# A decoder layer on one core: the second norm in a written order, and the first gate/up pair from eight block products

## The chip, the cores and the metric

The kernel runs on one NeuronCore of a Trainium2 chip. The metric is the device time of one execution in microseconds (us), lower is better. Five engines work side by side, each through its own list of instructions in order: TensorE (PE; its weight loads are shown as PEld), VectorE (DVE), ScalarE (ACT), GpSimd (POOL) and SyncE (SP), which starts most loads. They wait for each other by semaphores.

## What is computed

One layer of a decoder with 512 positions and a model width of 1024, all in float32:

```
h = rms_norm(x, attn_pre_norm) @ w_in          # split over four kinds of attention, 4 heads each
mix = concatenate([moba, nsa, diff, swa])      # 512 x 1024
x = x + rms_norm(mix @ w_out, attn_post_norm)
h = rms_norm(x, ffn_pre_norm)                  # "the second norm", with the line above
a = causal_conv3(h @ w_gate) + conv_b          # width 4096
x = x + rms_norm((gelu(a) * (h @ w_up)) @ w_down, ffn_post_norm)
```

## The kernel before

Every matrix product is made from float32r operands that are split into a high half (an ACT copy) and a low half (the difference, mostly on DVE), and three matmuls, high x high, high x low and low x high (`mm3`, L396). The weights come in by DMA and are split just ahead of their use; class `Weights` hands their steps to a queue (`later`, `pop`) that is emptied one step at a time between matmuls. The 512 positions are four tiles `t` of 128 rows, the width 1024 two halves `n` of 512.

**Out-projection.** The first half of its depth is made inside the attention (`fill_out`) and copied into `part[t][n]`. The other half needs the last heads: `out_rest(t, n)` (L1162) makes 12 matmuls of 512 columns into one PSUM bank and DVE adds the bank to `part` (L1168). The mixed heads reach it as `mixh` (ACT, L950) and `mixl` (POOL, L951); the last `mixl` ends the attention.

**Second norm** (`second_norm`, L1188; `rstd2`, L1170). Per tile: ACT squares `part` with a running sum, DVE adds the sums, POOL raises to -0.5; `part` is multiplied by the first gain (DVE for tile 0, POOL for the others), DVE multiplies by `r` and adds to `x1` (L1195), then squares, `r` and product with the second gain once more (L1198). `x1` is loaded again from memory by ACT's queue (L1155).

**Gate and up.** 32 column tiles of 128 each are made in 16 pairs. A pair is a product of a 2 x 2 block matrix (weights) with a 2 x 2 block matrix (normed rows, transposed), done by seven block products of 24 matmuls of 256 columns instead of eight; POOL makes the combinations of the weight blocks (L167) and DVE and ACT those of the results (`first_products`, `other_products`). The right operands are the normed rows: `"11"` and `"21"` hold tiles 0 and 1 (first and second 512 features), `"12"` and `"22"` tiles 2 and 3, and `t1` to `t4` are combinations of them (`other_operands`, L1231). `right_operand` (L1200) makes one: eight TensorE transposes, two ACT copies, two DVE subtractions. In front of the rest, `first_products` of pairs 0 and 1 use only `"21"` and `"11"`. Weight operands are split into buffers `wu`; the first two, four halves in all, go to buffers called `wa`.

A scheduler orders each engine's instructions from the program's order, its own estimate of times and priorities (`tc.high_priority`).

## Time and profile before

| | us |
|---|---|
| runs, median of 3 (lowest to highest) | 824.68 (823.82 to 824.93) |
| the profiled execution | 825.51 |
| its span, from the first to the last instruction | 823.7 |
| TensorE busy in the span | 781.1 |
| DVE busy | 659.4 |
| ACT busy | 445.5 |
| POOL busy | 345.2 |

Times in rows are counted from the start of the span. A busy matmul is counted to its modelled end, so neighbours overlap: what a matmul costs is the distance of its start to the next one's start. The order of rows below stands without times, as the program was built.

### The profile page before, as it was taken

The page shows a single profiled execution, that of the slowest core. Times are in us where ns is not written, and L with a number is a line of the kernel's source. Part 1 is how long each engine was busy: PE and PEld are TensorE (multiplying, and loading weights), DVE is VectorE, ACT ScalarE, POOL GpSimd, SP SyncE. Part 2 cuts the span into 40 slices and gives each one's busy share as a digit, 9 for nine tenths or more (in the row PEclk, how much of TensorE's full clock was granted, in tenths as well). Part 3 has the DMA queues.
Part 4 walks back from the last instruction along what each step waited for, and adds up shares of the span by engine and source line. Part 5 has one row for each costly group of instructions (what it writes and reads, how often), then busy time and mean ns, then how long its engine had stood idle before and what let it go on. Part 6 is the DMA issues. An engine that isn't in the chain of part 4 may idle for free.

```text
span 823.7 us, 13488 instructions
## 1 busy us (share of the span) xinstructions
PE 781.1 (95%) x5079; PEld 711.5 (86%) x5079; DVE 659.4 (80%) x1124; ACT 445.5 (54%) x930; POOL 345.2 (42%) x312
## 2 busy tenths in 40 slices
PE   7999998999999779999999999999999999999994
PEld 6998887998877569988998998998998998998983
DVE  4647669777686999995797797897897897899766
ACT  6457656776776535644554454454454454455432
POOL 5136342337344657333433432452451451564005
PEclk9999998999999969999999999999999999999998
DMA  7274211406321403422123314305306216123302
GB/s 225 52 200 128 58 40 45 125 24 204 105 70 56 148 17 113 128 78 77 52 80 125 103 51 155 103 25 182 96 12 200 72 32 204 29 75 103 102 27 102
DMA packets 72920, 78.76 MB, mean 96 GB/s; under 512 B 7782, under 2 KB 58136, under 8 KB 72856
## 3 DMA queue, kind: packets, MB, share of 16 engines
q1 hardware_dynamic: 70888, 73.18, 28.6%
q10 hardware_dynamic: 1968, 4.73, 1.6%
q8 instruction: 40, 0.66, 0.3%
q14 instruction: 24, 0.20, 0.1%
HBM read 73.71 MB, written 2.10 MB: 92 GB/s over the span
## 4 chain that ended last, share of the span: by engine, by line
PE 56%; DVE 32%; DMA 4%; issue 3%; ACT 3%; POOL 2%; SPq 0%; ACTq 0%; DVEq 0%; POOLq 0%
DVE wu L184 13%; PE mm L397 5%; PE mm L398 4%; PE mm L399 4%; PE tr L398 3%; DVE y L1313 3%; PE mm L1263 3%; PE mm L1265 3%; PE mm L1264 3%; PE tr L399 3%; PE sc L1265 3%; PE sc L1264 3%; PE sc L1263 3%; PE tr L397 3%; PE tr L924 2%
## 5 line engine op out<-in xcount | busy, mean ns | idle before, releaser
L184 DVE TENSOR_TENSOR wu<-pair,wu 128x512 fp32r<-128x512 f32 x188 | 176.1, 972 | 15.2 <-ACT wu L181 15.0
L181 ACT ACTIVATE wu<-pair 128x512 fp32r<-128x512 f32 x188 | 108.3, 622 | 74.8 <-PE sc L1265 19.6
L1265 PE MATMUL mm<-fT,wu 128*128 128x256 f32 x488 | 138.3, 283 | 0.7 <-DVE wu L184 0.7
L1263 PE MATMUL mm<-fT,wu 128*128 128x256 f32 x488 | 138.2, 283 | 0.7 <-ACT mo L1294 0.7
L1264 PE MATMUL mm<-fT,wu 128*128 128x256 f32 x488 | 138.2, 283 | 0.0
L142 ACT ACTIVATE wu<-raw 128x512 fp32r<-128x512 f32 (+2 forms) x126 | 71.3, 610 | 78.3 <-DMA raw<-in_ffn_w_down_dram 28.5
L1264 PE MATMUL sc<-fT,wu 128*128 128x256 f32 x392 | 111.3, 284 | 0.0
L1263 PE MATMUL sc<-fT,wu 128*128 128x256 f32 x392 | 111.1, 284 | 0.0
L1265 PE MATMUL sc<-fT,wu 128*128 128x256 f32 x392 | 111.1, 283 | 0.0
L167 POOL TENSOR_TENSOR sum<-pair 128x512 f32<-128x512 f32 x32 | 48.4, 1515 | 140.0 <-DMA pair<-in_ffn_w_up_dram 63.4
L167 POOL TENSOR_TENSOR pair<-sum,pair 128x512 f32<-128x512 f32 x32 | 55.9, 1761 | 117.5 <-DVE wu L184 115.7
L167 POOL TENSOR_TENSOR pair<-pair 128x512 f32<-128x512 f32 x64 | 103.9, 1634 | 2.0
L147 DVE TENSOR_TENSOR wu<-raw,wu 128x512 fp32r<-128x512 f32 (+2 forms) x95 | 67.6, 727 | 38.7 <-ACT wu L142 38.3
L1263 PEld LDWEIGHTS mm<-fT,wu 128*128 128x128 f32 x488 | 93.6, 192 | 1.2 <-ACT mo L1294 0.9
L1265 PEld LDWEIGHTS mm<-fT,wu 128*128 128x128 f32 x488 | 93.6, 192 | 0.9 <-DVE wu L184 0.9
L1264 PEld LDWEIGHTS mm<-fT,wu 128*128 128x128 f32 x488 | 93.6, 192 | 0.3
L1263 PEld LDWEIGHTS sc<-fT,wu 128*128 128x128 f32 x392 | 75.4, 193 | 0.4
L1264 PEld LDWEIGHTS sc<-fT,wu 128*128 128x128 f32 x392 | 75.3, 192 | 0.3
L1265 PEld LDWEIGHTS sc<-fT,wu 128*128 128x128 f32 x392 | 75.3, 192 | 0.0
L892 POOL TENSOR_SCALAR P<-P,rc 128x128 f32<-128x128 f32 (+2 forms) x80 | 43.0, 558 | 75.6 <-DVE rc L990 29.5
L147 POOL TENSOR_TENSOR wu<-raw,wu 128x512 fp32r<-128x512 f32 (+2 forms) x31 | 42.0, 1359 | 55.4 <-ACT wu L142 50.4
L900 ACT ACTIVATE P<-P,mn 128x128 f32<-128x128 f32 (+2 forms) x96 | 52.0, 543 | 21.5 <-DVE mn L899 21.0
(312 smaller groups left out, 1998.6 us busy)
## 6 DMA issues: line engine op xcount, KB each, us to landing
pair<-in_ffn_w_gate_dram SPq DMA_DIRECT2D x16, 1024.0 KB
pair<-in_ffn_w_up_dram SPq DMA_DIRECT2D x16, 1024.0 KB, 5.3
raw<-in_ffn_w_down_dram SPq DMA_DIRECT2D x32, 512.0 KB, 3.8
raw<-in_w_in_dram SPq DMA_DIRECT2D x14, 512.0 KB, 3.7
raw<-in_w_out_dram SPq DMA_DIRECT2D x8, 512.0 KB, 4.2
raw<-in_w_in_dram SPq DMA_DIRECT2D x10, 256.0 KB, 2.7
x<-in_x_dram SPq DMA_DIRECT2D x4, 512.0 KB, 6.2
x<-in_x_dram ACTq DMA_DIRECT2D x4, 512.0 KB, 8.6
```

Of the source, the lines that this page charges most:

```text
L142: self.nc.scalar.activation(box["h"][:, sl], box["r"][:, sl], AF.Copy)
L147: eng.tensor_tensor(box["l"][:, sl], box["r"][:, sl], f32(box["h"][:, sl]), op=ALU.subtract)
L167: self.nc.gpsimd.tensor_tensor(block(g, out), block(g, a), block(g, b), op=op)
L181: self.nc.scalar.activation(box["h"][g], block(g, src), AF.Copy)
L184: self.nc.vector.tensor_sub(box["l"][g], block(g, src), f32(box["h"][g]))
L397: pe.matmul(o, lh, rh, start=first, stop=False)
L398: pe.matmul(o, lh, rl, start=False, stop=False)
L399: pe.matmul(o, ll, rh, start=False, stop=last)
L900: act.activation(pi, pi, AF.Exp, bias=mn[:, i:i + 1], scale=-1.0, accum_out=sm[:, i:i + 1])
L1263: pe.matmul(o, wh, rh, start=first, stop=False, skip_group_check=True)
L1264: pe.matmul(o, wh, rl, start=False, stop=False, skip_group_check=True)
L1265: pe.matmul(o, wl, rh, start=False, stop=last, skip_group_check=True)
```

## The change

- Pair 0 is made from its plain blocks. `add_blocks` splits four operands (11, 12, 21, 22) and no combination of weights; `block_products` makes eight products straight into four PSUM banks, in two rounds, `a = 0` for tiles 0 and 1, `a = 1` for tiles 2 and 3. Pair 1 still takes seven products and comes after pair 0.
- The out-projection's rest, the second norm, the transposes and the products of pair 0 are issued in a written order, which `tc.keep_in_program_order` holds on every engine. `out_rest` is finished one half after the other, tiles 0 and 1 first. The scalar steps of the norm are two POOL operations per norm, the first gain is POOL's for `n = 0` and DVE's for `n = 1`.
- The weights `wa` are split earlier (`ask_ahead`), inside the attention; three instead of four buffers of pair weights are loaded at first; `x1` is loaded by SP's queue.
- Lines move: L167 of before is L174, L184 is L191, L899 is L907, L924 is L932, L951 is L959, L956 is L964; the out-projection is L1196, its add L1198, the gain L1216, the residual L1222, the second product L1227, transposes and low halves of operands L1241 and L1244, block products L1393.

The core of the diff:

```diff
 class Weights:
@@
-        self.spare, self.held = {}, 0
+        self.spare, self.held, self.ahead = {}, 0, set()
+        self.keep = lambda i: i
@@
-    def add_operands(self, u, js, q, late=False):
-        for j in js:
+    def add_operands(self, u, q):
+        for j in range(7):
             n = len(self.units)
-            self.units.append(lambda j=j, n=n: self.operand(u, j, n, q, late))
+            self.units.append(lambda j=j, n=n: self.operand(u, j, n, q, OPERANDS, 6))
+
+    def add_blocks(self, u, q):
+
+        for j in range(4):
+            n = len(self.units)
+            self.units.append(lambda j=j, n=n: self.operand(u, j, n, q, BLOCKS, 3))
 
     def open_pairs(self, pool):
         self.big = pool
-        self.room["pair"] = PAIRS
+        self.room["pair"] = PAIRS - 1
         self.pump()
@@
+    def ask_ahead(self):
+
+        self.ahead = set(self.spare)
+        for u in sorted(self.ahead):
+            self.later(*self.units[u]())
...
@@
+    pair_units(0, W.add_blocks)
+    pair_units(1, W.add_operands)
...
@@
         W.spare = {u: lambda: [tt("wa", "H") for _ in range(2)] for u in W.spare}
+        W.ask_ahead()
         for n in range(2):
@@
+    keep = tc.keep_in_program_order
     x1 = [fp.tile([128, D], F32, name=f"x1_{t}") for t in range(4)]
     for t in range(4):
-        act.dma_start(x1[t], x[0, 128 * t:128 * t + 128, :])
+        sp.dma_start(x1[t], x[0, 128 * t:128 * t + 128, :])
+    W.done("pair")
@@
+    def out_rest(t, n):
+        ps = bank(("mm", "sc")[n])
+        sl = slice(128 * t, 128 * t + 128)
+        for k in range(4):
+            w = ws[2 * n + k // 2]
+            for a, c in ((0, 0), (0, 1), (1, 0)):
+                keep(pe.matmul(ps, mixT[a][4 + k][:, sl], w[c][:, k % 2, :], start=k == 0 and a == c == 0,
+                               stop=k == 3 and a == 1))
+        return lambda: keep(vec.tensor_add(part[t][n], part[t][n], ps))
+
+    def squares(t, n, src):
+
+        if n == 0:
+            rms[t] = (st.tile([128, 2], F32, tag="ssa", name=nm("ss")), st.tile([128, 1], F32, tag="ra", name=nm("r")))
+        ss, r = rms[t]
+        junk = acts.tile([128, 1024], BF16, tag="mo", name=nm("junk"), bufs=MO)
+        keep(act.activation(junk[:, 0:512], src, AF.Square, scale=1.0 / 32, accum_out=ss[:, n:n + 1]))
+        if n == 0:
+            keep(pool.tensor_scalar(r, ss[:, 0:1], 1.0, EPS, ALU.mult, ALU.add))
+        else:
+            keep(pool.tensor_tensor(r, r, ss[:, 1:2], op=ALU.add))
+            keep(pool.tensor_tensor(r, r, mhalf[:, 0:1], op=ALU.pow))
+
+    def first_gain(t, n):
+        keep((pool, vec)[n].tensor_tensor(part[t][n], part[t][n], half_of(gpost, n), op=ALU.mult))
+
+    def residual(t):
+        r = rms[t][1]
         for n in range(2):
             xh = half_of(x1[t], n)
-            vec.scalar_tensor_tensor(xh, part[t][n], r, xh, ALU.mult, ALU.add)
-        r = rstd2(x1[t])
+            keep(vec.scalar_tensor_tensor(xh, part[t][n], r, xh, ALU.mult, ALU.add))
+            squares(t, n, xh)
+
+    def second_norm(t):
         for n in range(2):
-            vec.scalar_tensor_tensor(part[t][n], half_of(x1[t], n), r, half_of(gpre, n), ALU.mult, ALU.mult)
...
+            keep(vec.scalar_tensor_tensor(part[t][n], half_of(x1[t], n), rms[t][1], half_of(gpre, n),
+                                          ALU.mult, ALU.mult))
...
@@
+    half_done(0, 0)
+    half_done(0, 1)
+    residual(0)
+    half_done(1, 0)
+    half_done(1, 1)
+    second_norm(0)
+    residual(1)
+    for n in range(2):
+        for t in (2, 3):
+            adds[t, n] = out_rest(t, n)
+        W.free(2)
+    half_done(2, 0)
+    half_done(3, 0)
+    second_norm(1)
+    R["11"] = right_operand([part[0][0], part[1][0]], operand_tiles("M"), keep)
+    R["21"] = right_operand([part[0][1], part[1][1]], operand_tiles("M"), keep)
+    half_done(2, 1)
+    residual(2)
+    for _ in range(4):
+        pop()
+    half_done(3, 1)
+    residual(3)
+    second_norm(2)
+    for _ in range(4):
+        pop()
+    second_norm(3)
@@
-    firsts = [first_products(tag) for tag in ("mm", "sc")]
-    with tc.high_priority(HN):
-        other_operands()
+    def block_products(j, a, hold):
+
+        wh, wl = first_ws[j]
+        rh, rl = R[("11", "21", "12", "22")[2 * a + j % 2]]
+        for g in range(2):
+            o = first_banks[j // 2, g][:, 256 * a:256 * a + 256]
+            for k in range(4):
+                for n, (l, r) in enumerate(((wh, rh), (wh, rl), (wl, rh))):
+                    hold(pe.matmul(o, l[g][:, k, :], r[k], start=j % 2 == 0 and k == 0 and n == 0,
+                                   stop=j % 2 == 1 and k == 3 and n == 2))
+                if side and a:
+                    pop()
+
+    first_ws = [W.take() for _ in range(4)]
+    first_banks = {(f, g): bank(("mm", "sc")[f]) for f in range(2) for g in range(2)}
+    for j in range(4):
+        if j == 3:
+            R["12"] = right_operand([part[2][0], part[3][0]], operand_tiles("F"), keep)
+            R["22"] = right_operand([part[2][1], part[3][1]], operand_tiles("X"), keep)
+        block_products(j, 0, keep)
...
+    for j in range(4):
+        block_products(j, 1, keep)
+        name, src = others[j]
+        R[name] = right_operand(src, late[name], keep)
+        if j % 2:
+            W.free(2)
+            pend.append(gate_and_up(j // 2, first_banks[j // 2, 0], first_banks[j // 2, 1]))
+    pend += pair_of_tiles(1)
```

How the order moves, at three places.

The end of the attention, DVE and TensorE. `P`, `sc`, `mn`, `rc`, `sm` are softmax tiles, `mo` a pair of heads, `wa` the two early weight operands. DVE before, in a row:

```order
L879 RECIPROCAL rc_2675<-rc_2675 128x4
L899 ISA P_2667,mn_2668<-sc_2707,sbias,nsink 128x256
L899 ISA mn_2668 128x1
L1030 TENSOR_SCALAR rc_2675<-rc_2675,nlam 128x4
L946 TENSOR_TENSOR mo_2695<-vb_2686,tmp_2696 64x512
L899 ISA P_2667,mn_2668<-sc_2715,sbias,nsink 128x256
L899 ISA mn_2668 128x1
L1033 SCALAR_TENSOR_TENSOR P_2507<-P_2590,rc_2675,P_2507 128x128
```

and now:

```order
L191 TENSOR_TENSOR wa_2686<-pair_0_2636,wa_2684 128x512
L191 TENSOR_TENSOR wa_2687<-pair_1_2638,wa_2685 128x512
L907 ISA P_2665,mn_2666<-sc_2712,sbias,nsink 128x256
L907 ISA mn_2666 128x1
L907 ISA P_2665,mn_2666<-sc_2721,sbias,nsink 128x256
L907 ISA mn_2666 128x1
L886 TENSOR_SCALAR rc_2673<-sm_2592 128x4
L954 TENSOR_TENSOR mo_2699<-vb_2690,tmp_2700 64x512
L887 RECIPROCAL rc_2673<-rc_2673 128x4
L191 TENSOR_TENSOR wa_2742<-pair_0_2636,wa_2740 128x512
L1038 TENSOR_SCALAR rc_2673<-rc_2673,nlam 128x4
L191 TENSOR_TENSOR wa_2743<-pair_1_2638,wa_2741 128x512
```

Four subtractions of `wa` stand among the softmax steps; before they stood behind the attention's last row. TensorE before (`kk` and `kl` with `qs` make scores, `mm` is the out-projection's bank):

```order
L956 MATMUL sc_2707<-kk_2657,qs_2383 128x256
L957 MATMUL sc_2707<-kl_2631,qs_2383 128x256
L956 MATMUL sc_2715<-kk_2657,qs_2383 128x256
L957 MATMUL sc_2715<-kl_2631,qs_2383 128x256
L956 MATMUL sc_2738<-kk_2657,qs_2392 128x128
L957 MATMUL sc_2738<-kl_2631,qs_2392 128x128
L399 MATMUL mm_3179<-wu_2957,mixl_2552 128x512
L399 MATMUL mm_3193<-wu_2957,mixl_2552 128x512
L956 MATMUL sc_2759<-kk_2657,qs_2392 128x256
```

and now:

```order
L964 MATMUL sc_2712<-kk_2655,qs_2383 128x256
L965 MATMUL sc_2712<-kl_2631,qs_2383 128x256
L964 MATMUL sc_2721<-kk_2655,qs_2383 128x256
L965 MATMUL sc_2721<-kl_2631,qs_2383 128x256
L1196 MATMUL mm_3169<-wu_2971,mixl_2552 128x512
L964 MATMUL sc_2748<-kk_2655,qs_2392 128x128
L965 MATMUL sc_2748<-kl_2631,qs_2392 128x128
L964 MATMUL sc_2769<-kk_2655,qs_2392 128x256
L965 MATMUL sc_2769<-kl_2631,qs_2392 128x256
```

The matmul with `mixl` stands ahead of one more pair of score matmuls, and belongs to one output half instead of two.

The gate/up products, TensorE: the transposes for tiles 2 and 3 (`part` with numbers 2938, 3010 before; 2952, 3024 now). Before, in the middle of a product:

```order
L1264 MATMUL sc_3482<-fT_3308,wu_3413 128x256
L1265 MATMUL sc_3482<-fT_3307,wu_3413 128x256
L1208 MATMUL tr_3550<-ident,part_2938 128x128
L1263 MATMUL sc_3482<-fT_3298,wu_3413 128x256
L1264 MATMUL sc_3482<-fT_3299,wu_3413 128x256
L1265 MATMUL sc_3482<-fT_3298,wu_3413 128x256
L1263 MATMUL sc_3482<-fT_3298,wu_3413 128x256
L1264 MATMUL sc_3482<-fT_3299,wu_3413 128x256
L1265 MATMUL sc_3482<-fT_3298,wu_3413 128x256
L1208 MATMUL tr_3550<-ident,part_3010 128x128
```

and now, where the third block ends:

```order
L1393 MATMUL sc_3434<-fT_3341,wu_3392 128x256 x2
L1393 MATMUL sc_3434<-fT_3342,wu_3392 128x256
L1393 MATMUL sc_3434<-fT_3341,wu_3392 128x256
L1241 MATMUL tr_3511<-ident,part_2952 128x128
L1241 MATMUL tr_3511<-ident,part_3024 128x128
L1241 MATMUL tr_3511<-ident,part_2952 128x128
L1241 MATMUL tr_3511<-ident,part_3024 128x128
L1241 MATMUL vb_3518<-ident,part_2952 128x128
```

Sixteen transposes now stand in a row ahead of the fourth block; before, products stood between them.

The second norm of tiles 2 and 3, DVE (`x_2`, `x_3` are the residuals of those tiles, `part` the rows, `fT` low halves of right operands, `wu` low halves of weights). Before:

```order
L1195 SCALAR_TENSOR_TENSOR x_3_3171<-part_3010,r_3392,x_3_3171 128x512
L1195 SCALAR_TENSOR_TENSOR x_3_3171<-part_3160,r_3392,x_3_3171 128x512
L1211 TENSOR_TENSOR fT_3281<-tr_3275,fT_3280 128x512
L1211 TENSOR_TENSOR fT_3290<-vb_3284,fT_3289 128x512
L1211 TENSOR_TENSOR fT_3299<-tr_3293,fT_3298 128x512
L1181 TENSOR_SCALAR r_3382<-ss_3379 128x1
L1211 TENSOR_TENSOR fT_3308<-va_3302,fT_3307 128x512
L1181 TENSOR_SCALAR r_3402<-ss_3399 128x1
L1198 SCALAR_TENSOR_TENSOR part_2938<-x_2_3170,r_3382,gains 128x512
L1198 SCALAR_TENSOR_TENSOR part_3109<-x_2_3170,r_3382,gains 128x512
L1198 SCALAR_TENSOR_TENSOR part_3010<-x_3_3171,r_3402,gains 128x512
L1198 SCALAR_TENSOR_TENSOR part_3160<-x_3_3171,r_3402,gains 128x512
```

and now:

```order
L191 TENSOR_TENSOR wu_3392<-pair_0_2636,wu_3392 128x512
L191 TENSOR_TENSOR wu_3392<-pair_1_2638,wu_3392 128x512
L1198 TENSOR_TENSOR part_3148<-part_3148,sc_3310 128x512
L1216 TENSOR_TENSOR part_3148<-part_3148,gains 128x512
L1222 SCALAR_TENSOR_TENSOR x_3_3159<-part_3024,r_3332,x_3_3159 128x512
L1222 SCALAR_TENSOR_TENSOR x_3_3159<-part_3148,r_3332,x_3_3159 128x512
L1227 SCALAR_TENSOR_TENSOR part_2952<-x_2_3158,r_3383,gains 128x512
L1227 SCALAR_TENSOR_TENSOR part_3123<-x_2_3158,r_3383,gains 128x512
L191 TENSOR_TENSOR wu_3416<-pair_0_2636,wu_3416 128x512
L191 TENSOR_TENSOR wu_3416<-pair_1_2638,wu_3416 128x512
L1227 SCALAR_TENSOR_TENSOR part_3024<-x_3_3159,r_3405,gains 128x512
L1227 SCALAR_TENSOR_TENSOR part_3148<-x_3_3159,r_3405,gains 128x512
```

Tile 3's add, gain and residual stand behind the weight halves that follow tile 2's residual; before both residuals stood together, ahead of the low halves of tiles 0 and 1.

## Rows read from the trace of the kernel before

**Rows 1.** Page, engines: busy us (share of the span), instructions.

```profile
PE 781.1 (95%) x5079; PEld 711.5 (86%) x5079; DVE 659.4 (80%) x1124; ACT 445.5 (54%) x930; POOL 345.2 (42%) x312
```

**Rows 2.** Stretches: window, its length, busy us of each engine (instructions), clock, DMA share, GB/s.

```profile
230.00:269.50 39.50, 35.99 (x223) 29.82 (x223) 28.69 (x92) 28.92 (x81) 20.55 (x28) 1.00 0.23 68
269.50:298.50 29.00, 17.56 (x74) 13.38 (x72) 28.97 (x40) 15.29 (x35) 20.05 (x17) 0.81 0.23 90
...
365.00:800.00 435.00, 431.20 (x2928) 399.13 (x2927) 366.70 (x478) 208.68 (x365) 163.10 (x100) 1.00 0.29 94
```

**Rows 3.** TensorE's waits, 230 to 420 us: total, times, longest us.

```profile
PE tr L1208 <- DVE part L1198: 10.0, 2, 6.6
...
PE tr L1208 <- DVE r L1181: 1.0, 1, 1.0
...
PE mm L1263 <- ACT mo L1294: 0.7, 1, 0.7
...
PE vb L1208 <- DVE fT L1211: 0.4, 1, 0.4
```

**Rows 4.** POOL in order of time: start, us, line, operation [idle before].

```profile
268.23 1.30 POOL L951 TENSOR_TENSOR mixl<-mo,mixh 128x512 fp32r<-128x512 f32 x1 [2.64 <-ACT mixh L950]
...
277.13 1.30 POOL L1192 TENSOR_TENSOR part<-part,gains 128x512 f32<-128x512 f32 x1
...
286.81 0.54 POOL L1182 TENSOR_TENSOR r<-r,mhalf 128x1 f32<-128x1 f32 x1 [2.61 <-DVE r L1181]
```

**Rows 5.** TensorE in order of time, out-projection's end, first product, transposes.

```profile
282.65 0.39 PE L398 MATMUL sc<-wu,mixh 128*128 128x512 f32 x1
282.88 0.39 PE L399 MATMUL sc<-wu,mixl 128*128 128x512 f32 x1
...
298.54 0.79 PE L1263 MATMUL mm<-fT,wa 128*128 128x256 f32 x2
...
313.30 0.28 PE L1265 MATMUL sc<-fT,wu 128*128 128x256 f32 x1
313.42 0.28 PE L1263 MATMUL sc<-fT,wu 128*128 128x256 f32 x1
313.54 0.60 PE L1208 MATMUL tr<-ident,t 128*128 128x128 f32 x4
313.89 0.36 PE L1264 MATMUL sc<-fT,wu 128*128 128x256 f32 x1
```

**Rows 6.** DVE in order of time, 269 to 300 us.

```profile
269.30 1.98 DVE L184 TENSOR_TENSOR wa<-pair,wa 128x512 fp32r<-128x512 f32 x3 [1.81 <-ACT wa L181]
...
277.28 3.40 DVE L1195 SCALAR_TENSOR_TENSOR x<-part,r,x 128x512 f32<-128x512 f32 x2
...
285.26 1.40 DVE L1195 SCALAR_TENSOR_TENSOR x<-part,r,x 128x512 f32<-128x512 f32 x2
286.59 0.14 DVE L1181 TENSOR_SCALAR r<-ss 128x1 f32<-128x1 f32 x1
...
298.86 0.68 DVE L1211 TENSOR_TENSOR fT<-tr,fT 128x512 fp32r<-128x512 f32 x1
```

**Rows 7.** ACT in order of time, 268 to 273 us.

```profile
268.63 2.20 ACT L181 ACTIVATE wa<-pair 128x512 fp32r<-128x512 f32 x4 [0.48 <-issue]
272.09 0.63 ACT L1176 ACTIVATE junk<-part 128x512 bf16<-128x512 f32 x1 [1.26 <-DVE part L1168]
272.63 0.19 ACT L1176 ACTIVATION_READ_ACCUMULATOR junk<-part 128x1 f32 x1
```

**Rows 8.** Page, DMA issues: KB each, median us to landing.

```profile
x<-in_x_dram ACTq DMA_DIRECT2D x4, 512.0 KB, 8.6
```

**Rows 9.** Stretches of 1 and 2 us; the clock is third from the end.

```profile
288.00:290.00 2.00, 0.16 (x1) 0.16 (x2) 2.00 (x4) 2.00 (x6) 0.90 (x1) 0.50 0.00 0
132.00:133.00 1.00, 0.00 (x0) 0.00 (x0) 0.97 (x4) 0.98 (x2) 0.01 (x1) 1.00 0.00 0
134.00:135.00 1.00, 0.98 (x5) 0.56 (x4) 1.00 (x3) 1.00 (x4) 0.00 (x0) 0.54 0.99 318
```

More of the change, by code (lines that the diff above doesn't have):

```diff
@@ L180, in hi @@
                                            for a in range(2)] for t in self.slot(n))
-            self.nc.scalar.activation(box["h"][g], block(g, src), AF.Copy)
+            self.keep(self.nc.scalar.activation(box["h"][g], block(g, src), AF.Copy))
         def lo(g):
-            self.nc.vector.tensor_sub(box["l"][g], block(g, src), f32(box["h"][g]))
+            self.keep(self.nc.vector.tensor_sub(box["l"][g], block(g, src), f32(box["h"][g])))
             if g == 1:
                 self.ready[n] = (box["h"], box["l"])
-            if j == 6:
+            if j == last:
                 self.done("pair")
         steps = [lambda: hi(0), lambda: hi(1), lambda: lo(0), lambda: lo(1)]
-        sums = [lambda g=g, m=m: combine(g, *m) for m in (
-            ("s", "21", "22", ALU.add), ("21", "11", "21", ALU.subtract),
-            ("11", "s", "11", ALU.subtract), ("12", "12", "11", ALU.subtract)) for g in range(2)]
-        if j == 2 and late:
-            return sums + steps
-        return steps + sums if j == 1 and not late else steps
+        if j == 1 and srcs is OPERANDS:
+            steps += [lambda g=g, m=m: combine(g, *m) for m in (
+                ("s", "21", "22", ALU.add), ("21", "11", "21", ALU.subtract),
+                ("11", "s", "11", ALU.subtract), ("12", "12", "11", ALU.subtract)) for g in range(2)]
+        return steps
     def ask(self):
@@ L201, in ask @@
             self.split += 1
-            self.later(*self.units[self.split - 1]())
+            if self.split - 1 not in self.ahead:
+                self.later(*self.units[self.split - 1]())
+    def ask_ahead(self):
+        self.ahead = set(self.spare)
+        for u in sorted(self.ahead):
+            self.later(*self.units[u]())
     def take(self):
@@ L285, with sum_tile @@
     W.later, W.pop = later, pop
-    def sum_tile(late):
-        t = tf("sum") if late else wst.tile([128, S], F32, tag="sum", name=nm("sum"), bufs=2)
+    def sum_tile():
+        t = wst.tile([128, S], F32, tag="sum", name=nm("sum"), bufs=2)
         return t.rearrange("p (k c) -> p k c", k=4)
@@ L1160, with half_of @@
     ws = [W.take() for _ in range(4)]
[L1162 to L1168 removed]
+    def half_of(a, n):
+        return a[:, 512 * n:512 * n + 512]
     def rstd2(*src):
@@ L1200, in right_operand, with operand_tiles @@
-    def right_operand(src, tags, tag):
+            keep(vec.scalar_tensor_tensor(part[t][n], half_of(x1[t], n), rms[t][1], half_of(gpre, n),
+                                          ALU.mult, ALU.mult))
+    def operand_tiles(tag):
+        return [t2pool.tile([128, S], F32R, tag="X", name=nm("fT")) if tag == "X" else tt("fT", tag) for _ in range(4)]
+    def right_operand(src, tiles, hold):
         hi, lo = [], []
         for m in range(2):
-            ps = bank(tags[m])
+            ps = bank(("tr", "pv")[m])
@@ L1207, in right_operand @@
                     c = 128 * (2 * m + k)
-                    pe.transpose(ps[:, 256 * k + 128 * u:256 * k + 128 * u + 128], src[u][:, c:c + 128], ident)
-            h, l = (t2pool.tile([128, S], F32R, tag="X", name=nm("fT")) if tag == "X" else tt("fT", tag) for _ in range(2))
-            act.activation(h, ps, AF.Copy)
-            vec.tensor_sub(l, ps, f32(h))
+                    hold(pe.transpose(ps[:, 256 * k + 128 * u:256 * k + 128 * u + 128], src[u][:, c:c + 128], ident))
+            h, l = tiles[2 * m:2 * m + 2]
+            hold(act.activation(h, ps, AF.Copy))
+            hold(vec.tensor_sub(l, ps, f32(h)))
             for k in range(2):
```

103 lines of the change are left out of this document (39 added, 64 removed).

## The prediction

> **What bounds the kernel now.** I read the page's table of engines first, then the stretches, then the waits of TensorE, then single rows in order of time. TensorE is the busiest engine [rows 1], and the stretches say where it is not: from 365 us to 800 it works 431.2 of 435 us, but from 269.5 to 298.5, the second norm, only 17.6 of 29 [rows 2]. The reader is to see two regimes there: a feed-forward part in which every matmul more is paid in full, and a hole of 11.4 us ahead of it in which DVE is busy all the time (28.97 of 29). The waits name the hole: TensorE's transposes of the normed rows (L1208) wait 10.0 us for DVE's L1198, and 1.0 us for a small DVE operation [rows 3]. So only three things can move the time: the matmuls that TensorE has to do, the end of the attention, and the wait between that and the first gate/up product.
>
> I count from M, the end of the last low half of the attention's output (POOL L951, 268.23 + 1.30 = 269.5 us [rows 4]). TensorE starts the first product at 298.54 [rows 5], that is M + 29.0.
>
> **More matmuls.** Pair 0 takes eight block products instead of seven: 24 matmuls of 256 columns more. Two of them in a row start 0.12 us apart (313.30, 313.42): 2.9 us. There are also eight right operands to transpose instead of seven; four transposes take 0.35 us of TensorE (313.54 to 313.89), so eight take 0.7 [rows 5]. All of it lies on the engine that is full: **+3.6**. What pair 0 loses on other engines (eight POOL combinations, five DVE sums, two ACT copies, three weight operands to split) hides beside TensorE before and is worth nothing, but for a wait of 0.7 us on one of those copies (L1294), and a 0.4 us wait on an fT low half in the same stretch, which I expect gone [rows 3]: **-1.1** (bounds -1.1 and 0).
>
> **The end of the attention.** The four halves of two operands called wa were split behind the attention: four ACT copies from 268.63, 2.20 us, and four DVE subtractions, 1.98 us for the first three [rows 6, 7]. Now they stand between the last softmax tiles (first fences of order). Ahead of M, DVE and ACT are busy 28.7 and 28.9 of 39.5 us, 73% [rows 2]. Four subtractions at 0.66 (1.98 / 3) are 2.6; at that share 1.9 us lie on the chain of softmax steps. Worst is copies and subtractions one behind the other, 4 x (0.55 + 0.66) = 4.8. Best is a gain: out-projection matmuls that stood ahead of the last value products no longer do; the twelve of one output half at 0.23 us (282.65 to 282.88 [rows 5]) are 2.8 us, so -2.8. I take **+1.9**, by the row of DVE's share. The four loads of x1 go from ACT's queue to SP's; they land 8.6 us after issue [rows 8], and are first wanted some 7 us behind M while issued about 3 ahead of it, so I cost them at nothing; should they be late, every us is paid at the first norm. SP has them ahead of the second half of pair 1's weights, which nobody needs before pair 1's combinations.
>
> **The first norm.** The out-projection's rest was done for several output tiles side by side, which filled TensorE's gaps in the attention; now each of the eight halves is finished before the next begins. The first half can't end before M, and the other seven follow: 84 x 0.23 = 19.3, with the first half's last matmul M + 19.6. Meanwhile tiles 0 and 1 go through DVE, ACT and POOL. Tile 1's second half leaves TensorE at M + 8.7; add 0.7, square 0.63 + 0.19 [rows 7], two small POOL operations at 0.54 [rows 4] behind a POOL gain of 1.3, residual 1.4 for two [rows 6], two squares 1.6, POOL 1.1, two products 1.4: about M + 17.5, inside the cover. So TensorE goes from the out-projection straight to the transposes, and the first product stands at 19.6 + 0.35 + 0.55 + 0.68 = M + 21.2 (a bank's four transposes, ACT's copy at 2.20 / 4, DVE's low half [rows 6, 7]). Against 29.0: **-7.8**. If the chain is stretched as DVE's steps were beside POOL's gains (below), it is later by 2 to 4 us: bounds -7.8 and -4.
>
> **What is late next: tiles 2 and 3.** On TensorE the transposes of tiles 2 and 3 stand in a row between block 2 and block 3 (second fences), so nothing passes them. Three blocks, 72 matmuls at 0.12, last to 21.2 + 8.6 = M + 29.8. On DVE the order is now fixed (third fences): the four low halves of tiles 0 and 1 end at about M + 22.2 (sixteen transposes are 1.4, a copy and a low half 1.2), and only then tile 2's second half is added. From there one step waits for the next: add 0.7, square 0.8, POOL 1.1, residual 1.4 (M + 26.2); a square 0.8 on ACT, behind it two weight copies 1.1, then the second weight subtraction 0.7 on DVE (28.8); tile 3's add 0.7, square 0.8, POOL 1.1, residual 1.4 (32.8); last square 0.8, two weight copies 1.1, two weight subtractions 1.3, two products 1.4: M + 37.4 (the last POOL pair runs beside the weight halves). Some fifteen hand-overs between engines come on top; DVE's r ends at 286.73 and POOL starts at 286.81 [rows 4, 6], 0.08 each, 1.2 in all: M + 38.6. TensorE waits 38.6 - 29.8 = **+8.8**, first for the third block's weights, then for tile 3. Before, TensorE waited nowhere in this stretch, since two product groups ran while tiles 2 and 3 were normed. Bounds: 1.5, if the scalar steps overlap far better than this row by row sum; 12, if two residuals take 3.40 us instead of 1.40, as they did beside POOL's gains (277.28, 285.26 [rows 6]).
>
> That last pair of rows shows DVE's step as long as POOL's gain of 1.30 and the one after it. The Trainium skill (SBUF — State Buffer, section "SBUF: two separate sides") calls the port that the two share an exclusive lock held for a whole instruction, and the rows agree (1.40 against 3.40). By that rule the chain of tiles 2 and 3 is free of it, since POOL then has only operations of one column, and 8.8 stands; without the rule it would be 8.8 + 2 x 2.0.
>
> **The sum.** +3.6 - 1.1 + 1.9 - 7.8 + 8.8 = +5.4. The profiled execution of before took 825.51 us (span 823.7, 1.8 around it), so 830.9; it lies 0.8 above the median of the three runs, 824.68, which gives **830.1**.
>
> TensorE's clock is at its lower level (0.50, 1.2 GHz) from 288 us on [rows 9], after the long wait; the new wait of about 9 us would cost the same, so I put no term. But TensorE fell to it at 134.5 too, having stood still from 132 to 133 [rows 9].
>
> **Rivals.**
> Faster: the norms of tiles 2 and 3 overlap and TensorE waits only 1.5 us. For it: DVE has less to do in the stretch than before (no sums of pair 0, POOL fewer gains), and the scalar steps are on three engines. Against it: the fixed order puts one tile behind the other. +3.6 - 1.1 + 1.9 - 7.8 + 1.5 = -1.9, 822.8.
> No change: a wait of 3.4 us, in the middle, 824.7.
> Much slower, by one mechanism: TensorE holds its out-projection matmuls in order inside the attention, stands before the low half of a mixed tile, and the score matmuls behind it (the first fences) come late. The attention's chain has hardly slack, so the stall of some 2 us is paid, and the clock falls as at 134.5; six us at half clock would cost up to 3. It decides as soon as that low half is later than the row of matmuls, and gives 830.1 + 5 = 835.1. The Trainium skill (TensorE: Matmul & The Clock Gate, section "HAM oscillation — how this bites in real kernels") says that waits between bursts bring the slow clock back each time; the drop at 134.5 agrees.
>
> **Chances.** Forecast 0.55; much slower 0.20; faster 0.16; no change 0.09. 0.2% (1.6 us) is about what a measurement of this kernel can tell from no change. Of the forecast's own range, 826.5 to 833.5, all is slower. The range reaches to the faster case's centre and just past the slowest's: 822.5 to 836. Faster by over 0.2% 0.16, within 0.09, slower 0.75.
>
> **What would show it.** First product behind the last L951 (now L959) by 21 to 23 us instead of 29.0; 24 matmuls and 8 transposes more; TensorE's waits in 290 to 320 us on DVE's L1227 (second norm of tiles 2 and 3) and on DVE's L191 (third block's weights), 6 to 11 us together; M itself at 270 to 273 us. The forecast is wrong if those waits are under 3 us, or if M comes earlier than 269.

## The result, and the profile after

| | median us | lowest to highest (runs) | profiled run, us | its span | mean clock |
|---|---|---|---|---|---|
| before | 824.93 | 823.82 to 827.91 (5) | 825.51 | 823.7 | 0.983 |
| changed | 833.48 | 833.24 to 835.09 (5) | 833.24 | 831.5 | 0.976 |

The changed kernel takes 1.0094 times as long (95% interval 1.0072 to 1.0116): 8.5 us by the medians, 7.8 by the two spans. The forecast was 5.4 more. The direction is the forecast's, the size 3 us more: 833.48 lies at the upper end of the forecast's own range of 826.5 to 833.5.

The page's engines, and stretches that answer to [rows 1, 2]; the first two are cut at the ends of the attention and of the second norm as they lie now, the third is as long a stretch behind the first product:

```profile
PE 789.9 (95%) x5111; PEld 720.8 (87%) x5111; DVE 650.2 (78%) x1111; ACT 443.1 (53%) x932; POOL 332.6 (40%) x316
```

```profile
230.00:272.70 42.70, 32.58 (x186) 26.58 (x184) 32.20 (x95) 29.60 (x81) 20.52 (x28) 0.88 0.22 68
272.70:295.40 22.70, 22.68 (x101) 18.83 (x102) 11.75 (x17) 7.81 (x23) 11.46 (x18) 0.92 0.29 106
295.40:330.00 34.60, 26.95 (x186) 25.42 (x184) 29.52 (x37) 14.68 (x32) 17.86 (x18) 0.85 0.29 92
365.00:800.00 435.00, 432.70 (x2969) 401.53 (x2968) 371.22 (x483) 211.32 (x369) 167.63 (x102) 1.00 0.29 94
```

The hole of the second norm is closed: TensorE works 22.68 of 22.70 us there, where it had 17.56 of 29.00. But the third row is new. Behind the first product TensorE loses 7.65 us and its clock is 0.85 on the mean, and in the attention the clock is 0.88 where it was 1.00. The same length behind the first product before, where it lost 1.23 us:

```profile
298.50:333.10 34.60, 33.37 (x263) 32.43 (x264) 33.78 (x44) 16.43 (x30) 23.82 (x16) 0.96 0.30 93
```

TensorE's waits, 230 to 420 us, answering to [rows 3] (total, times, longest):

```profile
PE tr L1241 <- DVE part L1227: 4.5, 2, 3.3
PE sc L964 <- DVE mn L907: 2.5, 3, 1.1
PE tr L932 <- DVE P L1041: 1.9, 1, 1.9
PE mm L1196 <- ACT mixh L958: 1.6, 1, 1.6
PE sc L1393 <- ACT wu L188: 1.5, 1, 1.5
PE mm L1196 <- POOL mixl L959: 1.3, 2, 0.7
...
PE tr L1241 <- DVE part L1419: 0.7, 1, 0.7
PE tr L1241 <- DVE part L1417: 0.7, 1, 0.7
```

The two rows of 10.0 and 1.0 us are gone. In their place stand 4.5 us for the second products of tiles 2 and 3, 1.5 for the third block's weights, and small waits in the attention.

To set kernels side by side in spite of a start that differs from run to run, I count from the fifth low half of the attention's output, which all of them reach with nearly the same code. It starts at 239.62 before:

```profile
239.62 1.29 POOL L951 TENSOR_TENSOR mixl<-mo,mixh 128x512 fp32r<-128x512 f32 x1
```

and now, with the last low half, which answers to the first of [rows 4]:

```profile
238.74 1.28 POOL L959 TENSOR_TENSOR mixl<-mo,mixh 128x512 fp32r<-128x512 f32 x1
...
271.38 1.28 POOL L959 TENSOR_TENSOR mixl<-mo,mixh 128x512 fp32r<-128x512 f32 x1 [2.19 <-ACT mixh L958]
```

The span then has three pieces: fifth to last low half (A), last low half to first gate/up product (B), that product to the end (C). All are differences of starts in the profiled executions, C from the first product to the end of the page's span, to about 0.1 us:

| run | A | B | C | median us |
|---|---|---|---|---|
| before | 28.6 | 30.3 | 525.2 | 824.9 |
| changed | 32.6 | 24.1 | 536.1 | 833.5 |
| e1, wa behind | 29.4 | 23.3 | 536.2 | 833.2 |
| e2, loose out-projection | 35.0 | 19.8 | 535.2 | 832.0 |
| e3, block first | 32.6 | 23.9 | 537.0 | 835.6 |
| e4, a block less | 33.5 | 23.3 | 535.4 | 834.7 |
| e5, two tiles | 33.9 | 23.4 | 532.7 | 831.1 |
| e6, POOL later | 32.3 | 23.8 | 533.0 | 832.3 |
| e7, e5 + e6 | 34.1 | 23.5 | 528.7 | 828.3 |
| e8, e7 + e1 + e3 | 31.1 | 23.6 | 529.2 | 826.2 |
| e9, e7 + e1 | 29.5 | 24.8 | 528.4 | 826.6 |
| e10, e9, a block less | 31.6 | 24.0 | 531.9 | 829.1 |
| e11, e9 + e2 | 28.6 | 20.7 | 531.0 | 821.1 |
| e12, e11 + e3, weights later | 28.6 | 21.1 | 529.8 | 822.7 |

So the change costs 4.0 in A, gives 6.3 in B and costs 10.9 in C. A alone spreads by about 2 us between runs with the same code up to there (32.3 in e6, 34.1 in e7; 29.4 in e1, 31.6 in e10). For the second pair the traces show what differs: around 242 us TensorE has waits of the same lengths in all four (1.3 and 0.4 us), but its clock falls there in e8 and e10 and does not in e1 and e9. e1, then e10:

```profile
242.00:249.00 7.00, 5.99 (x36) 4.41 (x37) 6.68 (x27) 4.97 (x19) 1.74 (x4) 1.00 0.01 3
```

```profile
242.00:249.00 7.00, 6.55 (x26) 4.90 (x25) 5.70 (x21) 4.36 (x17) 1.73 (x4) 0.52 0.04 17
```

So a difference in A is read only where groups of runs don't overlap. Beside the experiments the kernel before took 826.0 to 826.6 us by the median; their ratios are to those runs, and a difference of 1 us or so between medians of two rows says little.

### The profile page after: what moved, and what is told of

It is laid out like the page before. It is cut to its first block, busy times and chain, and to the rows that moved or that the text cites. A ratio compares the mean times of both kernels' runs of the same rounds, so it can differ in the third digit from the quotient of the medians.

```text
span 831.5 us, 13566 instructions
## 1 busy us (share of the span) xinstructions
PE 789.9 (95%) x5111; PEld 720.8 (87%) x5111; DVE 650.2 (78%) x1111; ACT 443.1 (53%) x932; POOL 332.6 (40%) x316
## 3 DMA queue, kind: packets, MB, share of 16 engines
q1 hardware_dynamic: 71464, 75.28, 29.4%
## 4 chain that ended last, share of the span: by engine, by line
PE 44%; DVE 15%; issue 2%; POOL 1%; DMA 1%; ACT 1%; DVEq 0%; POOLq 0%
DVE wu L191 8%; PE mm L1304 4%; PE mm L1303 4%; PE mm L1302 4%; PE tr L405 4%; PE tr L406 3%; PE sc L1302 3%; PE sc L1304 3%; PE sc L1303 3%; PE tr L404 3%; DVE y L1354 2%; PE vb L404 2%; PE vb L406 2%; PE vb L405 2%; PE va L404 2%
## 5 line engine op out<-in xcount | busy, mean ns | idle before, releaser
L191 DVE TENSOR_TENSOR wu<-pair,wu 128x512 fp32r<-128x512 f32 x184 | 168.2, 951 | 17.8 <-ACT wu L188 17.6
L188 ACT ACTIVATE wu<-pair 128x512 fp32r<-128x512 f32 x184 | 106.2, 622 | 70.2 <-PE mm L1304 14.0
L1304 PE MATMUL mm<-fT,wu 128*128 128x256 f32 x480 | 135.9, 283 | 0.0
L1302 PE MATMUL mm<-fT,wu 128*128 128x256 f32 x480 | 135.9, 283 | 0.0
L1303 PE MATMUL mm<-fT,wu 128*128 128x256 f32 x480 | 135.8, 283 | 0.0
L174 POOL TENSOR_TENSOR sum<-pair 128x512 f32<-128x512 f32 x30 | 45.7, 1528 | 148.7 <-DMA pair<-in_ffn_w_up_dram 58.9
L1304 PE MATMUL sc<-fT,wu 128*128 128x256 f32 x360 | 101.9, 283 | 0.0
L1303 PE MATMUL sc<-fT,wu 128*128 128x256 f32 x360 | 101.9, 283 | 0.0
L1302 PE MATMUL sc<-fT,wu 128*128 128x256 f32 x360 | 101.8, 283 | 0.0
L174 POOL TENSOR_TENSOR pair<-pair 128x512 f32<-128x512 f32 x60 | 97.8, 1644 | 1.7
L174 POOL TENSOR_TENSOR pair<-sum,pair 128x512 f32<-128x512 f32 x30 | 53.4, 1798 | 112.0 <-DVE wu L191 112.0
L1303 PEld LDWEIGHTS mm<-fT,wu 128*128 128x128 f32 x480 | 92.1, 192 | 0.3
L1302 PEld LDWEIGHTS mm<-fT,wu 128*128 128x128 f32 x480 | 92.1, 192 | 0.3
L1304 PEld LDWEIGHTS mm<-fT,wu 128*128 128x128 f32 x480 | 92.1, 192 | 0.3 <-DVE wu L191 0.2
L1302 PEld LDWEIGHTS sc<-fT,wu 128*128 128x128 f32 x360 | 69.1, 192 | 0.4
L1303 PEld LDWEIGHTS sc<-fT,wu 128*128 128x128 f32 x360 | 69.1, 192 | 0.4
L1304 PEld LDWEIGHTS sc<-fT,wu 128*128 128x128 f32 x360 | 69.1, 192 | 0.0
```

The source lines that it names most:

```text
L174: self.keep(self.nc.gpsimd.tensor_tensor(block(g, out), block(g, a), block(g, b), op=op))
L188: self.keep(self.nc.scalar.activation(box["h"][g], block(g, src), AF.Copy))
L191: self.keep(self.nc.vector.tensor_sub(box["l"][g], block(g, src), f32(box["h"][g])))
L1302: pe.matmul(o, wh, rh, start=first, stop=False, skip_group_check=True)
L1303: pe.matmul(o, wh, rl, start=False, stop=False, skip_group_check=True)
L1304: pe.matmul(o, wl, rh, start=False, stop=last, skip_group_check=True)
```

## The experiments

**e1: wa behind the attention.** Where did A's 4.0 us come from?

```diff
-        W.ask_ahead()
+        pass
```

> The changed kernel with the four halves of the two operands wa split behind the attention again, as in the kernel before; all else as changed. Theory A, the splits in the softmax stage made the end of the attention late: the last low half (L959) ends at 269.5 to 270.3 us instead of 272.7, TensorE does not stand still from 242 to 244.5, the clock stays at 1.00 from 242 to 249, and the time falls by 2 to 3.5 us to 830.0 to 831.5; the tile norms behind lose nothing, since DVE stands idle from 270.6 to 273.3. Rival B, the held out-projection matmuls made it late (the wait for mixl at 240.07): L959 still ends at 272 or later and the time stays within 1 us of 833.5. Rival C, the splits cost as much behind the attention as in it: L959 early, but the first block product no earlier than 294.5 and the time above 832.5.

The last low half, fifth and eighth rows of L959 in e1:

```profile
238.94 1.26 POOL L959 TENSOR_TENSOR mixl<-mo,mixh 128x512 fp32r<-128x512 f32 x1
...
268.32 1.28 POOL L959 TENSOR_TENSOR mixl<-mo,mixh 128x512 fp32r<-128x512 f32 x1 [2.19 <-ACT mixh L958]
```

29.4 us instead of 32.6: in the traced execution theory A's mechanism holds, with 829.55 us, just below its range. The other four executions took 833.16 to 833.29 at a mean clock of 0.972 to 0.976 (0.984 in the traced one), so the median is the changed kernel's. Alone, the edit is worth 3.3 us of A in one execution and nothing in the time of four. The later runs say more: the four traces with wa behind the attention and TensorE held (e1, e8, e9, e10) have an A of 29.4 to 31.6, the six with wa ahead (changed, e3 to e7) 32.3 to 34.1, and no two overlap. What the other four of e1 lost is not shown; a fall of the clock near 242, as in e8 and e10, is a candidate. On top of e7 the edit is worth 1.7 (e9) by the medians.

**e2: the out-projection not held.** Is the held order of TensorE a gain?

```diff
-                keep(pe.matmul(ps, mixT[a][4 + k][:, sl], w[c][:, k % 2, :], start=k == 0 and a == c == 0,
-                               stop=k == 3 and a == 1))
+                pe.matmul(ps, mixT[a][4 + k][:, sl], w[c][:, k % 2, :], start=k == 0 and a == c == 0,
+                          stop=k == 3 and a == 1)
```

> The changed kernel with the out-projection's matmuls of the second half not held in a written order on TensorE; the adds, norms and blocks behind them stay held. The matmuls of the first four halves then stand in the attention's last gaps again. Theory A, the seven halves behind the attention are paid in full and the hold costs more than it gives: behind the last L959 only the last part of four halves and four whole halves are left (16 matmuls and 48, 64 x 0.23 = 14.7 us against 19.3 us), the first block product comes 16 to 19 us behind L959 instead of 22.8, bound by DVE's chain of tile 1, and the time falls by 3 to 6 us to 827.5 to 830.5. Rival B, the out-projection is only cover for the norms of tiles 0 and 1: first product still 21 to 23 us behind L959, time 832.5 to 834. Rival C, the hold in the attention made its end late (waits on mixl): the last L959 itself moves from 272.7 to 271 or earlier.

B falls to 19.8 as theory A said, but A grows by 2.3, so the median is only 1.4 lower and the time misses theory A's. Rival C is refuted here: without the hold the attention ends no earlier (35.0 lies just above the 34.1 of e7, so how much later stays open). Together with e1's edit it will be another matter (e11).

**e3: the fourth block first.** Can a block fill the hole before tile 3?

```diff
-    for j in range(4):
-        if j == 3:
+    for j in range(5):
+        if j == 4:
...
-        block_products(j, 0, keep)
+        j < 4 and block_products(j, 0, keep)
```

> The changed kernel with the fourth plain block (tiles 0 and 1) put ahead of the transposes of tiles 2 and 3 on TensorE. Theory A, the hole is tile 3's norm and the fourth block can stand in it: its weights (L191) end at 311.35, so its 24 matmuls run from there to about 314.3 while tile 3's second product ends at 314.7; of the hole 2.9 us are filled and the time falls by 2.5 to 4.5 us (more, if the clock stays up) to 829.0 to 831.0. Rival B, the hole only moves: DVE's low halves and late combinations are as late as before and TensorE waits for them in front of the blocks of tiles 2 and 3 (waits on L1244, L1417, L1419 together up by 2 us or more); time 832.5 or more.

Its waits, 230 to 345 us:

```profile
PE sc L1393 <- ACT wu L188: 4.7, 2, 3.2
PE tr L1241 <- DVE part L1417: 4.2, 2, 2.9
```

The 4.5 us for L1227 are gone and came back as 3.2 for the fourth block's weights and 4.2 for DVE's late combinations. Rival B: the hole only moves. C is 0.9 longer, and the median 2.1. What binds is the chain over DVE and ACT (which copies the weights), not the order of the blocks on TensorE.

**e4: a block less.** It leaves out the last of the eight plain blocks.

```diff
-        block_products(j, 1, keep)
+        j < 3 and block_products(j, 1, keep)
```

> The changed kernel with the last of the eight plain blocks (24 matmuls of 256 columns, fourth weights times the last quarter of the rows of tiles 2 and 3) left out of the computation; its eight right operands are still made. Theory A, every matmul of this stretch is paid in full: 24 x 0.12 = 2.9 us less, 830.3 to 831.0. Rival B, the block stands beside DVE's combinations and low halves, which bind there: 0 to 1 us less, 832.5 to 833.5, and TensorE waits in the stretch from 320 to 345 for DVE instead.

C falls by 0.7, not 2.9, and the median is 834.7, no lower than the changed kernel's. Its waits in the same stretch:

```profile
PE tr L1241 <- DVE part L1227: 5.8, 2, 3.2
...
PE tr L1241 <- DVE part L1419: 1.8, 2, 1.5
...
PE tr L1241 <- DVE part L1417: 1.3, 1, 1.3
```

These three are 3.0 us more than in the changed kernel (5.9). TensorE waits for what it no longer computes: rival B.

**e5: tiles 2 and 3 side by side.** The two norms' steps are interleaved, and the third block's weights split ahead.

```diff
+    for _ in range(4):
+        pop()
...
     half_done(2, 1)
-    residual(2)
-    for _ in range(4):
-        pop()
     half_done(3, 1)
+    residual(2)
+    for _ in range(2):
+        pop()
     residual(3)
+    for _ in range(2):
+        pop()
     second_norm(2)
-    for _ in range(4):
-        pop()
     second_norm(3)
```

> The changed kernel with tiles 2 and 3 normed side by side: the third block's weights are split behind tile 1's second product, both tiles' second halves are added one behind the other, then both residuals, the fourth block's weights, both second products. Theory A, one tile behind the other made tile 3 late: DVE stands idle less between 297 and 308 (0.85 + 0.71 + 1.37 + 0.85 + 0.71 us in the changed kernel), tile 3's second product ends 5 to 7 us earlier behind the first block product (13 to 14.5 us behind it instead of 19.3), and the time falls by 4 to 7 us to 826.5 to 829.5. Rival B, the hole only moves on to DVE's late combinations and low halves: TensorE's waits on L1417 and L1419 grow by 3 us or more and the time falls by 0 to 2 us, 831.5 to 833.5.

C falls by 3.4, the median by 2.4: between the two theories. Tile 3's products end 15.5 us behind the first product, not 13 to 14.5. Tile 3's products on DVE:

```profile
307.50 1.41 DVE L1227 SCALAR_TENSOR_TENSOR part<-x,r,gains 128x512 f32<-128x512 f32 x2
309.35 3.42 DVE L1227 SCALAR_TENSOR_TENSOR part<-x,r,gains 128x512 f32<-128x512 f32 x2 [0.44 <-POOL r L1213]
```

The same two instructions take 1.41 us for tile 2 and 3.42 for tile 3; the waits on L1227 stay at 4.5. Something else stretches them.

**e6: POOL's combinations later.** In the changed kernel, DVE and then POOL in order of time (the third row is as long as 277.28 in [rows 6]):

```profile
308.61 1.41 DVE L1227 SCALAR_TENSOR_TENSOR part<-x,r,gains 128x512 f32<-128x512 f32 x2
310.06 1.29 DVE L191 TENSOR_TENSOR wu<-pair,wu 128x512 fp32r<-128x512 f32 x2
311.27 3.43 DVE L1227 SCALAR_TENSOR_TENSOR part<-x,r,gains 128x512 f32<-128x512 f32 x2
...
317.81 2.49 DVE L191 TENSOR_TENSOR wu<-pair,wu 128x512 fp32r<-128x512 f32 x4
320.22 3.47 DVE L1417 TENSOR_TENSOR part<-part,part 128x512 f32<-128x512 f32 x2
323.62 1.75 DVE L1419 TENSOR_TENSOR part<-part,part 128x512 f32<-128x512 f32 x1
```

```profile
311.13 3.02 POOL L174 TENSOR_TENSOR sum<-pair 128x512 f32<-128x512 f32 x2
...
319.84 3.30 POOL L174 TENSOR_TENSOR pair<-sum,pair 128x512 f32<-128x512 f32 x2 [2.77 <-DVE wu L191]
323.11 3.42 POOL L174 TENSOR_TENSOR pair<-pair 128x512 f32<-128x512 f32 x2
```

The steps that split pair 1's first operands and combine its blocks now stand behind L1421, and a POOL operation ahead of them reads L1421's last result:

```diff
+    gate = st.tile([128, 1], F32, tag="gate", name="gate")
+    keep(pool.tensor_scalar(gate, p[1][1][:, 0:1], 1.0, 0.0, ALU.mult, ALU.add))
     W.limit = W.early + 6
     W.ask()
     while side:
         pop()
```

> The changed kernel with POOL's combinations of pair 1, and the splits of its first two operands, put behind DVE's late combinations (L1417 to L1421), with one small POOL operation that reads the last of these, so that POOL can't start before. Theory A, POOL's combinations stretch DVE's steps beside them: the two products of tile 3 take 1.4 us instead of 3.43, the first pair of late combinations 1.4 instead of 3.47, the next ones 0.69 instead of 1.75 and 1.78 (6 us of DVE in all), DVE is the engine that binds there, and the time falls by 3 to 5 us to 828.5 to 830.5. Rival B, POOL's combinations are then late themselves: TensorE waits for pair 1's operands (L188, L191) between 325 and 350, and the time is 832.5 or more. Rival C, POOL is not what stretches them: the two products still take over 3 us.

DVE in e6, the same steps (L1411, L1413 are L1417, L1419 of the changed kernel):

```profile
311.98 1.41 DVE L1227 SCALAR_TENSOR_TENSOR part<-x,r,gains 128x512 f32<-128x512 f32 x2
317.52 1.28 DVE L1411 TENSOR_TENSOR part<-part,part 128x512 f32<-128x512 f32 x2
318.72 0.68 DVE L1413 TENSOR_TENSOR part<-part,part 128x512 f32<-128x512 f32 x1
```

All three are back at what they take alone, as theory A had them: POOL is what stretches them. C falls by 3.1. But the edit does a second thing: the four subtractions that split pair 1's first weights (317.81) stood on DVE ahead of the late combinations and now stand behind them. From tile 3's products to the last late combination DVE took 18.5 us and takes 10.7; some 6.4 of that are the steps no longer stretched, 2.5 the four subtractions, less 1.0 of a new wait for ACT. No run parts the two, so the 3.1 in C is not POOL's alone. The median falls by only 1.2, with executions from 830.04 to 833.86: above theory A's range, and not settled by this run alone.

**e7: e5 and e6 in one kernel.**

> Both of the edits before in one kernel: tiles 2 and 3 side by side, and POOL's combinations of pair 1 behind DVE's late combinations. If both causes are real and lie on one chain, the gains add up: 6 to 10 us less than the changed kernel, 823.5 to 827.5, and TensorE waits under 3 us between 300 and 345. If the stretch has another bound behind (TensorE's clock, the blocks themselves), no more than the larger of the two gains: 827 or more.

C falls by 7.3, a little more than 3.4 + 3.1, and the median by 5.2 to 828.27 (ratio to before 1.0030, 1.0018 to 1.0041), more than 2.4 + 1.2: the two edits act on one chain and their gains add up. The 6 to 10 us and the wait of under 3 us were still missed: TensorE waits 3.5 us on L1227.

**e8, e9: with wa behind the attention, with and without e3's edit.**

> The kernel of the run before, with the fourth block of tiles 0 and 1 ahead of the transposes of tiles 2 and 3 and with the halves of wa split behind the attention as before the change. Theory A, every wait named so far is gone: the end of the attention 3 us earlier, TensorE busy from the first block product on; 9 to 13 us less than the changed kernel, 820.5 to 824.5, below the kernel before. Rival B, the eight blocks cost more than the whole rest gives back: no faster than the kernel before, 825 or more.

> The kernel with all four edits, but the fourth plain block back behind the transposes of tiles 2 and 3, as in the changed kernel. Theory A, once DVE's chain is short the place of that block is worth nothing (the stretch from the first block product to the end was 528.7 us without it and 529.2 with it): 528 to 529.5 us from the first block product to the end, median 824.5 to 827. Rival B, the block fills a wait: 2 us or more slower than the kernel with all four, 828 or more.

826.22 (ratio 1.0000, 0.9986 to 1.0014) and 826.57 (0.9999, 0.9988 to 1.0010): both equal to before, and the place of the fourth block is worth nothing here, as theory A of e9 had it. The 820.5 to 824.5 of e8's theory A were missed; its rival B holds.

**e10: e9 with the last block left out of the computation.**

> The kernel of the run before with the last of the eight plain blocks (24 matmuls of 256 columns) left out of the computation. In the changed kernel leaving it out gave nothing behind the first block product (536.07 to 535.37 us), since TensorE then waited for DVE instead. Theory A, with DVE's chain short TensorE is the bound and the block is paid in full: 24 x 0.12 = 2.9 us less from the first block product to the end, 2 to 3.5 us less in all. Rival B, DVE still binds there: 0 to 1 us less.

829.08, no faster than e9 with the block, outside both theories' times; ten of its twelve executions took 827.59 us or more, two 822.95 and 823.14, below all of e9's. The trace shows both theories at work, one behind the other. Pair 1's first matmul, e9 and then e10, and e10's next bank:

```profile
327.69 0.37 PE L1304 MATMUL mm<-fT,wu 128*128 128x256 f32 x1
```

```profile
325.79 0.35 PE L1304 MATMUL mm<-fT,wu 128*128 128x256 f32 x1
...
332.11 0.55 PE L1304 MATMUL sc<-fT,wu 128*128 128x256 f32 x1 [3.23 <-DVE y L1357]
```

The first products stand at 293.89 and 294.78, so pair 1 begins 33.8 us behind the first product in e9 and 31.0 in e10: up to there the block is paid in full, 2.8 us. Then TensorE arrives early at pair 0's gate, waits 3.2 us for DVE, and runs on at 1.2 GHz: the clock is 0.66 from 330 to 340 us (1.00 in e9). The 2.8 are lost again, and C is 3.5 longer than in e9.

**e11: e9 with the out-projection not held.**

> The kernel with two tiles side by side, POOL's combinations later and wa behind the attention (three edits), and with the out-projection's matmuls not held in an order on TensorE. Theory A, as in the run with only that edit: the first block product comes some 19 to 20 us behind the last low half instead of 23.5, but the out-projection's matmuls in the attention make its end 1 to 2.5 us later; net 1 to 3 us less, 822 to 825. Rival B, without the wa halves in the softmax stage the four wa splits on DVE now stand in front of the first add and the norm chain, so the first block product comes no earlier: time as the run with the three edits or above.

821.10, ratio 0.9930 (0.9911 to 0.9948): faster than both kernels, and by more than theory A gave: 5.5 us against e9 by the medians. In the two traces it is 2.7 (824.04 to 821.33), since e9's traced execution is the fastest of its twelve. A is 28.6 and B 20.7 (29.5 and 24.8 in e9), and C gives 2.6 of that back, most of it where the first product, begun with one matmul, waits for a low half:

```profile
290.56 5.89 PE L1395 MATMUL mm<-fT,wa 128*128 128x256 f32 x47 [1.57 <-DVE fT L1244]
```

The stretch 230 to 302.5, e9 first, then e11:

```profile
230.00:302.50 72.50, 64.39 (x365) 53.95 (x365) 53.58 (x125) 43.01 (x118) 35.88 (x51) 0.93 0.22 73
```

```profile
230.00:302.50 72.50, 60.45 (x365) 50.43 (x365) 56.84 (x130) 44.65 (x123) 39.04 (x56) 1.00 0.23 77
```

As many matmuls lie in it, but e9 spends 64.39 busy us on them at a clock of 0.93, e11 60.45 at 1.00. e9's clock falls (0.66 from 255 to 260 us, 0.50 from 270 to 275) beside two waits in the attention's last steps that e11 does not have, where out-projection matmuls fill such gaps and no wait from 246 to 277 us is over 1.0 us:

```profile
254.22 1.10 PE L1055 MATMUL vb<-pair,tmp 128*128 128x2 f32 x8 [1.85 <-ACT tmp L1052]
...
269.06 1.22 PE L1196 MATMUL mm<-wu,mixh 128*128 128x512 f32 x2 [1.61 <-ACT mixh L958]
```

With wa in the softmax stage (e2) the loose order didn't do this; the clock was 0.73 from 240 to 250 there too. That e9's other executions lose more to the clock fits their mean clocks (0.974 to 0.983, against 0.982 to 0.989 in e11), but no trace of them shows it.

**e12: e11 with the fourth block first and the third block's weights behind the low halves.**

> The kernel with the loose out-projection and the three edits, with the fourth plain block ahead of the transposes of tiles 2 and 3 and the third block's weights split behind the low halves of tiles 0 and 1 instead of ahead of them. In the run without these two edits TensorE waited 1.6 us for the low halves and 3.5 us (2.04 and 1.46) for the second products of tiles 2 and 3. Theory A, the block's 24 matmuls fill that second wait and the low halves are in time: 2 to 4.5 us less, 816.5 to 819.5. Rival B, the fourth block waits for its own weights (L191 there ends 300.6, some 3 us behind the third block) and DVE's late operands are no earlier: 0 to 1.5 us less, 819.5 to 821.5.

822.69 (0.9952, 0.9934 to 0.9970), not faster than e11 and above the ranges of both theories. C is 1.1 shorter, but the median is above. e11 stays the best.

## Why the prediction was right in direction and short in size

- **End of the attention, +1.9; measured +4.0 in A (3.1 in M, 269.5 to 272.7).** The mechanism is right: e1 gives 3.3 back in its trace, and the traces with and without the early splits don't overlap. The size is off because DVE's busy share stood for the price. Two of the four subtractions stand beside POOL's mixl (238.74) and take 2.41 us instead of 1.32, so all four take 3.7 instead of 2.6:

```profile
238.77 2.41 DVE L191 TENSOR_TENSOR wa<-pair,wa 128x512 fp32r<-128x512 f32 x2
...
243.97 1.92 DVE L1041 SCALAR_TENSOR_TENSOR P<-P,rc,P 128x128 f32<-128x128 f32 x4
```

  They push DVE's L1041, TensorE stands 1.9 us for it, and the clock falls:

```profile
240.00:242.00 2.00, 0.86 (x3) 0.48 (x3) 2.00 (x8) 1.99 (x5) 0.02 (x1) 1.00 0.69 245
242.00:244.00 2.00, 0.54 (x3) 0.30 (x2) 2.00 (x7) 1.31 (x6) 0.00 (x0) 0.71 0.02 7
244.00:246.00 2.00, 1.54 (x6) 0.82 (x6) 1.97 (x6) 0.00 (x0) 0.00 (x0) 0.50 0.00 0
```

  "I put no term" for the clock is the step that failed here: the sum prices a wait without the slow clock beside it. The splits are not the fall's only cause: without them the held order has it in e8 and e10 and not in e1 and e9, and without splits and hold (before, e11, e12) the clock is 1.00 there. In that sense the much slower rival had a part: TensorE did wait for mixl ahead of 240.07 (0.67 us), and e11 shows that the hold costs 5.5 us by the medians (826.57 to 821.10) and 2.7 in the traces, once wa is out of the way. In e2 alone it did not.
- **First norm, -7.8; measured -6.3 in B.** The first product, 298.54 in [rows 5] and 295.43 now (below), stands 22.8 us behind the end of L959, inside the 21 to 23 given; forecast 21.2. TensorE goes from the out-projection straight to the transposes, as said. What is missing is the clock again: 0.50 from 274 to 276 us, so the second of the out-projection's halves, its matmuls 0.43 apart there, takes longer than 12 x 0.23. (The terms for tile 1 add up to M + 18.1, not 17.5; that is still inside the cover.)

```profile
295.43 6.25 PE L1393 MATMUL mm<-fT,wa 128*128 128x256 f32 x48
```

- **x1 on SP's queue, 0; right.** The first residual waits 0.72 us for POOL's r, not for a load.
- **More matmuls +3.6, stalls -1.1, tiles 2 and 3 +8.8: +11.3; measured +10.9 in C.** The sum is right in part by luck, since its parts are not what I wrote. The wait of 8.8 is 6.2 (4.5 on L1227, 1.7 on the third block's weights), and L1227 and L191 together, which were to be 6 to 11, are 4.7. Both stalls are gone, but 0.7 + 0.7 on L1417 and L1419 are new. So TensorE's waits there grow by 6.5 (1.1 to 7.6), while behind 345 us they shrink by 2.3 (before, 3.8 below and 0.7 on L184; now 2.2):

```profile
PE tr L398 <- DVE wu L147: 3.8, 6, 1.1
```

```profile
PE tr L405 <- DVE wu L154: 2.2, 5, 0.7
```

  With +3.6 that is 7.8. The other 3.1 are, as an estimate, the slow clock: 0.85 against 0.96 over 34.6 us behind the first product is 3.8 us of full clock, some of it lost while TensorE stood anyway. "All of it lies on the engine that is full" fell in the changed kernel, where TensorE waits for DVE and the eighth block left out gives 0.7 us (e4). With DVE's chain short the price was right, 2.8 us up to pair 1 in e10, until TensorE met the next wait. Tile 3's products ended 42.0 us behind M instead of 38.6: 2.6 of that is a late start (the low halves below end at M + 24.9, not 22.2), and the chain from there took 0.8 more than its rows. POOL stretched its last two products by 2.0, so without POOL the sum of single rows was too long, not too short.

```profile
296.83 0.68 DVE L1244 TENSOR_TENSOR fT<-va,fT 128x512 fp32r<-128x512 f32 x1
```
- **"the chain of tiles 2 and 3 is free of it, since POOL then has only operations of one column": wrong.** POOL's combinations of pair 1 were free to start as soon as POOL had done its last r; I had counted pair 0, which has none now, and not what POOL does next. The rule of the Trainium skill (SBUF — State Buffer, section "SBUF: two separate sides") that I cited holds, and e6 agrees with it (1.41 against 3.43); I applied it to the wrong list of POOL's work. The part of C that e6 takes away is 3.1 (with the four subtractions moved), that of e5 3.4, both 7.3.
- What stays open: how e6's gain divides between POOL and the four subtractions; what four of e1's five executions lost that the traced one did not; and what decides whether the clock falls at 242 us in the held order without the early splits.

## What to carry to other kernels

Ask of each stretch which engine sets the pace before pricing an instruction there: 24 matmuls taken off TensorE gave nothing where it waited for DVE. A written order on one engine must be laid against what the other engines do when they run out of written work, POOL above all. Taken off where TensorE was full, they gave 2.8 us up to the next wait and lost them there: follow a gain to the next engine that binds. And a wait of TensorE such as the 1.9 us in the attention or the 3.2 us of e10 should be charged with the slow clock seen beside it, not only with itself.
